# Layer two's first weights split into an attention buffer, normalised rows scaled by ScalarE and transposed two tiles later, layer one's norm weights spread by a product

## The chip, the core and the metric

The kernel runs on one core of one Trainium2 chip. TensorE (PE) multiplies matrices and transposes, VectorE (DVE), ScalarE (ACT) and GpSimd (POOL) work element by element, and SyncE (SP) issues transfers (DMA) between the chip's main memory and the core's two memories: SBUF, 128 partitions wide, and PSUM, into which PE writes. ACT can issue transfers too. Each engine runs its own list of instructions in order, and waits on semaphores for what others make. The metric is the device time of one execution in microseconds (us), as the median of several runs.

## The reference

Two equal layers work on a stream `h` of 512 tokens by 1024 columns, in float32. Each normalises its input, projects it, runs three mixers, and adds the output projection of their results to the stream.

```
def rms_norm(x, g, eps=NORM_EPS):
    xf = x.astype(jnp.float32)
    y = xf * lax.rsqrt(jnp.mean(xf * xf, axis=-1, keepdims=True) + eps)
    return (y * g.astype(jnp.float32)).astype(x.dtype)
...
    h = x
    for l in range(DEPTH):
        xn = rms_norm(h, ln_g[l])
        proj = xn @ w_in[l]
        u_a, z_a, u_b, z_b, q_lat, kv_lat, k_rope, z_c = jnp.split(proj, pts, axis=-1)
        y_a = rwkv7_mix(u_a, ...)
        y_b = rms_norm(rglru_mix(u_b, ...), lru_out_g[l])
        y_c = rms_norm(mla_mix(q_lat, kv_lat, k_rope, ...), mla_out_g[l])
        y = jnp.concatenate([y_a * jax.nn.silu(z_a), y_b * jax.nn.silu(z_b), y_c * jax.nn.silu(z_c)], axis=-1)
        h = h + y @ w_out[l]
    return rms_norm(h, final_g)
```

The change concerns `rms_norm(h, ln_g[l])` of both layers, the first columns of `xn @ w_in[l]` of layer two, and the last part of `h + y @ w_out[l]` of layer one, which overlaps them.

## The kernel before

**Precision.** Every float32 operand of a large product is split in two: a rounded high part made on ACT (`copy`, line 141) and a residue made on DVE or POOL (lines 211 and 229 for weights and activations, 306 for the normalised input). `mm3` then issues three products for each pair (lines 233, 234 and 235). A weight of 128x512 is loaded by SP into a buffer `wr` (three of them), and split by `weights` into `wH` and `wL` (four each). A `wr` is free for the next load when both parts have been made.

**Start of layer one.** The stream is cut into four tiles of 128 tokens. `LO` sets the order in which SP's first loads are written: digits are tiles of `x`, `i` the identity matrix that transposes need, `g` the norm weights `ln_g[0]`, copied to all 128 partitions (512 KB), `u`, `w`, `y` the first three weights. A scheduler sets the final order on each queue. For each tile, ACT squares two halves of 512 columns and sums them (`h_half`, line 242), ACT and DVE make 1/rms from it (`h_rstd`, lines 246, 138 and 254 to 256), DVE multiplies each half by 1/rms and by the norm weights (line 298), PE transposes it in four blocks into PSUM (line 303), ACT makes the high part `xH` (141), DVE the residue `xL` (306).

**The seam.** The last of the three output projections (`out_proj` with `final`) goes over n = 0, 1, the two halves of the 1024 columns, and in each over the four tiles. `start` loads the residual of a tile and half from main memory into `hp` (line 446, three buffers). Twelve products of four weights make the tile's result in PSUM. `finish` adds the residual (line 461, DVE), writes the sum back to main memory for the next layer's residual (464, SP), squares it (242, ACT) and multiplies it by the next norm's weights (`norm_gain`, line 286: POOL for n = 0, DVE for n = 1). After a tile's second half `norm_tile` makes 1/rms, scales both halves on DVE (line 301), and has them transposed and split as above, between the products of the tiles that are left. Layer two begins with the column groups j = 12 and j = 0, each in two halves of the tokens (`proj` with `halves`), so that the first 256-wide products need tiles 0 and 1 alone. Their four weights go through `weights` like all others.

The buffers called `am` (two of 16 KB a partition) hold the first mixer's score matrices, and later layer one's attention queries.

## Time and profile before

| | us |
|---|---|
| median of 3 runs | 857.3 (856.71 to 858.69) |
| the profiled execution | 855.86 |
| its span from the first to the last instruction | 854.0 |
| first product of layer one (PE, line 233) starts at | 15.49 |
| last-projection products stop for transposes at about | 426.3 |
| first product of layer two starts at | 434.63 |
| layer two's half-width products end at about | 449.5 |

Times in the profile are us from the span's start. A row of the timeline gives start, duration, engine, line, operation, out<-in with shapes, how many instructions were merged, and in brackets how long the engine had been idle before and what ended that. SPq is a transfer's issue on SP. `acc`, `ps` and `ck` are PSUM buffers, `c`, `g`, `sm` and `hp` SBUF buffers, `dr` main memory. The clock granted to PE was 0.984 of full on average.

### The profile page before, as it was taken

What the parts mean: (1) busy time and instruction counts of PE and PEld (TensorE: products, weight loads), DVE (VectorE), ACT (ScalarE), POOL (GpSimd) and SP (SyncE); (2) the same over time, 40 slices, a digit from 0 to 9 for tenths busy, and PEclk for the clock granted to TensorE, in tenths of its full rate; (3) what the DMA queues carried; (4) which work ended last, traced back from release to release, by engine and by line L of the source; (5) the groups of instructions that cost most, each with busy time, mean ns of one, the idle gap of its engine ahead of it and who ended that gap; (6) DMA issues with size and microseconds to landing.
All of it is one profiled execution on the core that took longest, in us unless ns stands there. A gap on an engine that the chain in (4) does not pass through costs nothing.

```text
span 854.0 us, 15206 instructions
## 1 busy us (share of the span) xinstructions
PE 796.6 (93%) x5696; PEld 621.0 (73%) x5696; DVE 571.6 (67%) x1173; ACT 506.2 (59%) x990; POOL 325.7 (38%) x299
## 2 busy tenths in 40 slices
PE   4999999999879989999989999999998799999996
PEld 4878888877559867556778788888765697675674
DVE  5678777924886496774474966695367946877736
ACT  6667885656563536574467687846575435465644
POOL 0455557513352332012344556574143523310223
PEclk9999999999999999999999999999999899999999
DMA  7222224310123365123732233332101234731354
GB/s 245 96 74 84 72 93 136 117 51 27 32 77 97 124 197 184 51 87 99 268 124 90 75 99 101 98 111 94 29 25 41 81 107 129 241 114 50 111 173 162
DMA packets 49755, 91.08 MB, mean 107 GB/s; under 512 B 5520, under 2 KB 8336, under 8 KB 49680
## 3 DMA queue, kind: packets, MB, share of 16 engines
q1 hardware_dynamic: 49104, 89.05, 32.2%
q8 instruction: 45, 0.74, 0.4%
q10 hardware_dynamic: 576, 1.05, 0.3%
q14 instruction: 30, 0.25, 0.1%
HBM read 73.30 MB, written 16.78 MB: 105 GB/s over the span
## 4 chain that ended last, share of the span: by engine, by line
PE 69%; DVE 16%; ACT 8%; issue 3%; DMA 2%; POOL 1%; SPq 1%; ACTq 0%; DVEq 0%; POOLq 0%
PE acc L233 16%; PE acc L234 16%; PE acc L235 15%; PE acc L1058 4%; PE ck L1084 3%; ACT g L138 2%; PE ps L1076 2%; PE ps L687 1%; DVE g L681 1%; PE ps L611 1%; ACT UV L141 1%; ACT L136 1%; DVE wL L229 1%; PE ps L629 1%; PE ps L786 1%
## 5 line engine op out<-in xcount | busy, mean ns | idle before, releaser
L229 POOL TENSOR_TENSOR wL<-wr,wH 128x512 fp32r<-128x512 f32 (+1 forms) x126 | 169.7, 1350 | 290.0 <-ACT wH L141 266.0
L141 ACT ACTIVATE wH<-wr 128x512 fp32r<-128x512 f32 (+1 forms) x192 | 118.8, 622 | 140.6 <-PE acc L234 74.5
L233 PE MATMUL acc<-xH,wH 128*128 128x512 f32 (+1 forms) x496 | 192.7, 390 | 0.0
L234 PE MATMUL acc<-xL,wH 128*128 128x512 f32 (+1 forms) x496 | 189.7, 383 | 0.4 <-DVE xL L306 0.2
L235 PE MATMUL acc<-xH,wL 128*128 128x512 f32 (+1 forms) x496 | 189.1, 381 | 0.0
L233 PEld LDWEIGHTS acc<-xH,wH 128*128 128x128 f32 x496 | 94.3, 191 | 18.1 <-ACT xH L141 0.7
L235 PEld LDWEIGHTS acc<-xH,wL 128*128 128x128 f32 x496 | 94.3, 190 | 17.3
L234 PEld LDWEIGHTS acc<-xL,wH 128*128 128x128 f32 x496 | 94.4, 190 | 16.9 <-DVE xL L306 0.9
L229 DVE TENSOR_TENSOR wL<-wr,wH 128x512 fp32r<-128x512 f32 (+1 forms) x66 | 49.9, 760 | 72.8 <-ACT wH L141 72.7
L233 PE MATMUL acc<-wH,c 128*128 128x512 f32 x192 | 83.0, 432 | 2.6 <-DVE hp L428 1.3
L234 PE MATMUL acc<-wL,c 128*128 128x512 f32 x192 | 77.5, 404 | 0.5 <-DVE wL L229 0.5
L235 PE MATMUL acc<-wH,c 128*128 128x512 f32 x192 | 77.1, 402 | 0.0
L141 ACT ACTIVATE UV<-ps 64x512 f32<-64x512 f32 (+4 forms) x112 | 52.4, 494 | 30.9 <-PE ps L1076 22.6
L233 PEld LDWEIGHTS acc<-wH,c 128*128 128x128 f32 x192 | 36.7, 191 | 12.8 <-ACT c L141 3.0
L141 ACT ACTIVATE c<-g 128x512 fp32r<-128x512 f32 (+1 forms) x40 | 24.9, 630 | 34.3 <-DVE g L981 22.4
L138 ACT ACTIVATE c<-acc,sm 128x128 f32<-128x128 f32 (+3 forms) x64 | 33.6, 528 | 19.1 <-DVE sm L1060 18.8
L234 PEld LDWEIGHTS acc<-wL,c 128*128 128x128 f32 x192 | 36.9, 192 | 8.6 <-issue 1.4
L1058 PE MATMUL acc<-am,am 128*128 128x128 f32 (+3 forms) x128 | 42.3, 447 | 0.8 <-ACT c L138 0.8
L235 PEld LDWEIGHTS acc<-wH,c 128*128 128x128 f32 x192 | 36.8, 192 | 8.4 <-issue 0.5
L369 POOL TENSOR_TENSOR g<-g,g 128x512 f32<-128x512 f32 x24 | 32.1, 1338 | 24.1 <-ACT g L138 24.1
L136 ACT ACT_TABLE_LOAD x31 | 39.8, 1283 | 1.3 <-PEq L1214 0.7
L138 ACT ACTIVATE g<-g 128x512 f32<-128x512 f32 (+1 forms) x58 | 36.4, 627 | 4.6 <-DVE g L705 2.6
(222 smaller groups left out, 1592.4 us busy)
## 6 DMA issues: line engine op xcount, KB each, us to landing
wr<-in_wc_dram SPq DMA_DIRECT2D x116, 256.0 KB, 2.7
wr<-in_wo_dram SPq DMA_DIRECT2D x48, 256.0 KB, 3.4
hp<-dr SPq DMA_DIRECT2D x38, 256.0 KB, 3.2
dr<-hp SPq DMA_DIRECT2D x28, 256.0 KB, 2.1
dr<-g SPq DMA_DIRECT2D x16, 256.0 KB, 2.5
g<-dr SPq DMA_DIRECT2D x16, 256.0 KB, 3.6
wr<-in_wl_dram SPq DMA_DIRECT2D x16, 208.0 KB, 2.5
dr<-c SPq DMA_DIRECT2D x12, 256.0 KB, 3.4
```

The lines of the kernel that those rows point to most:

```text
L136: chained(A.preload_act_table_set(SETS[st]))
L138: chained(A.activation(out=out, in_=in_, func=func, **kw))
L141: i = A.activation(out=out, in_=in_, func=AF.Copy, **kw)
L229: (V if wn[0] % wmod[0] == 0 or wn[0] <= 4 else G).tensor_tensor(out=L, in0=raw, in1=f(H), op=ALU.subtract)
L233: PE.matmul(o, a[0], b[0], start=start, stop=False)
L234: PE.matmul(o, a[0], b[1], start=False, stop=False)
L235: PE.matmul(o, a[1], b[0], start=False, stop=stop)
L369: G.tensor_tensor(out=z, in0=z, in1=s, op=ALU.mult)
L611: PE.matmul(os[e][:, cp, :].rearrange("p (x s) -> p x s", x=2), bk[rr, ch, :, :].rearrange("p x s -> p (x s)"), ar[rr, :, ch * 64:(ch + 1) ...
L1058: PE.matmul(o[:, 0:n], qT[:, hd, qt * 128:n], K2[:, p, e, 0:n], start=True, stop=True)
L1076: PE.transpose(o[:, (qt - kt) * 128:(qt - kt + 1) * 128], Pm[p][e, qt][:, kt * 128:(kt + 1) * 128], ident)
L1084: i = PE.matmul(ot[e * 64:(e + 1) * 64, k2 * 128:T], Vt[:, k2, 2 * p + e, :], PT[:, 2 * (k2 % 2) + e, 0:(4 - k2) * 128], start=(k2 == 0), ...
```

## The change

Four things are changed.

1. **Layer one's norm weights.** `ln_g[0]` is loaded as one row of 4 KB, issued by ACT, as is the identity matrix. Two products of a row of 128 ones (`on1`, set by POOL) with the two halves of the row spread it over 128 partitions into the two `ck` banks of PSUM, where DVE reads it in the scaling (`norm_first`). `LO` is written in another order.
2. **Layer two's first weights.** `first_weights` loads the four weights of j = 12 and j = 0 into `wr`, and splits them, high parts on ACT and residues on POOL, into one `am` buffer, before the second half of layer one's last output projection. `proj` takes them from there.
3. **Scaling.** In the seam the multiplication of a tile's two halves by 1/rms moves from DVE (`tensor_scalar`) to ACT (`copy` with a scale).
4. **Transposes.** Those of tile tt stand after the products of tile tt + 2, those of tiles 2 and 3 after all.

```diff
--- before.py
+++ after.py
@@ -61,7 +61,7 @@
     ORD1 = "M0 L0 L1 C0 M1 C1 P0 L2 O0 M2 U1 O1 C2 U2 P1 L3 M3 C3 U0 P2 O2"
     ORD2 = "G0 U3 G1 P3 G2 Z0 Z1 O3 G3 X0 f4 V0 V1 Z2 Q0 Q1 f0 V2 V3 f1 Q2 Q3 J0 f2 J1 K0 f3 W0 K1 W1 f5 W2 W3"
     ORD3 = "B0 H0 H1 A2 H2 H3 A3 H4 H5 H6 H7 B1 N0 g0 g1 t0 t6 t1 t2 t4 t5 t3 t7 T0 R0 Y0 g2 g3 T1"
-    LO = "0ig12uw3yvcm"
+    LO = "g0i1uw2y3vcm"
     Q1 = "aoooottttaaaooookvvqvkqvkqkqqqqq"
     WA, WB, WC, WD = 1000, 2, 2, 5
 
@@ -159,7 +159,8 @@
 
     vecs = P1.tile([128, DEPTH, NV], F32, name="vecs")
     cmk = g2([128, 2, 128])
-    raws, gb0 = {}, c4([128, D])
+    raws, gb0, on1 = {}, c4([128, D]), g2([1, 128])
+    G.memset(on1, 1.0)
 
     def raw_weights(j, hf):
         raws[j, hf] = tl("wr", [128, 512], F32, bufs=3)
@@ -167,10 +168,10 @@
 
 
     loads = {
-        "i": lambda: nc.sync.dma_start(out=C[:, 0:128], in_=cst[:, 0:128]),
+        "i": lambda: nc.scalar.dma_start(out=C[:, 0:128], in_=cst[:, 0:128]),
         "v": lambda: nc.sync.dma_start(out=vecs, in_=vec),
         "c": lambda: nc.sync.dma_start(out=C[:, 128:NCST], in_=cst[:, 128:NCST]),
-        "g": lambda: nc.sync.dma_start(out=gb0, in_=ln_g[0].partition_broadcast(128)),
+        "g": lambda: nc.scalar.dma_start(out=gb0[0:1, :], in_=ln_g[0].unsqueeze(0)),
         "m": lambda: nc.sync.dma_start(out=cmk, in_=cst[:, NCST + 1280:NCST + 1536].rearrange("p (a b) -> p a b", a=2)),
         "u": lambda: raw_weights(12, 0),
         "w": lambda: raw_weights(12, 1),
@@ -285,26 +286,47 @@
         hg[tt, n] = g2()
         (G, V)[n].tensor_tensor(out=hg[tt, n], in0=h[tt][:, n * 512:(n + 1) * 512], in1=xn[l][2][:, n * 512:(n + 1) * 512], op=ALU.mult)
 
-    def norm_tile(l, tt):
-
-        xH, xL, gb = xn[l]
+    def norm_first(tt):
+
+        xH, xL, gb = xn[0]
         rs = h_rstd(tt)
         c = slice(tt * 128, (tt + 1) * 128)
         for j in range(2):
             p = ps([128, 4, 128])
-            if l == 0:
-                s = slice(512 * j, 512 * j + 512)
-                src = g2()
-                V.scalar_tensor_tensor(out=src, in0=h[tt][:, s], scalar=rs, in1=gb[:, s], op0=ALU.mult, op1=ALU.mult)
-            else:
-                src = hg[tt, j]
-                V.tensor_scalar(out=src, in0=src, scalar1=rs, scalar2=None, op0=ALU.mult)
+            src = g2()
+            V.scalar_tensor_tensor(out=src, in0=h[tt][:, 512 * j:512 * j + 512], scalar=rs, in1=gb[j], op0=ALU.mult, op1=ALU.mult)
             for k in range(4):
                 PE.transpose(p[:, k, :], src[:, k * 128:(k + 1) * 128], ident)
             xh = xH[:, 4 * j:4 * j + 4, c]
             hc[tt] = copy(xh, p)
             i = V.tensor_tensor(out=xL[:, 4 * j:4 * j + 4, c], in0=p, in1=f(xh), op=ALU.subtract)
         return i
+
+    def norm_scale(tt):
+        rs = h_rstd(tt)
+        for j in range(2):
+            copy(hg[tt, j], hg[tt, j], scale=rs)
+
+    def norm_transposes(l, tt):
+        xH, xL, _ = xn[l]
+        c = slice(tt * 128, (tt + 1) * 128)
+        for j in range(2):
+            p = ps([128, 4, 128])
+            for k in range(4):
+                PE.transpose(p[:, k, :], hg[tt, j][:, k * 128:(k + 1) * 128], ident)
+            xh = xH[:, 4 * j:4 * j + 4, c]
+            copy(xh, p)
+            V.tensor_tensor(out=xL[:, 4 * j:4 * j + 4, c], in0=p, in1=f(xh), op=ALU.subtract)
+
+    wfirst = {}
+
+    def first_weights(l):
+        W = tl("am", [128, 4, 2, 512], F32R, bufs=2)
+        for i, (j, hf) in enumerate(((12, 0), (12, 1), (0, 0), (0, 1))):
+            raw = tl("wr", [128, 512], F32, bufs=3)
+            nc.sync.dma_start(out=raw, in_=wc[l, j, :, 4 * hf:4 * hf + 4, :].rearrange("p k c -> p (k c)"))
+            split(raw, W[:, i, 0, :], W[:, i, 1, :], G)
+            wfirst[l, j, hf] = W[:, i, 0, :], W[:, i, 1, :]
 
     ov = out.rearrange("(n p) d -> p n d", p=128)
 
@@ -332,7 +354,8 @@
 
             if halves:
                 o = acc()
-                W = [weights(wc[l, j, :, 4 * hf:4 * hf + 4, :].rearrange("p k c -> p (k c)"), raw=raws.pop((j, hf), None)) for hf in range(2)]
+                W = [wfirst.pop((l, j, hf), None) or weights(wc[l, j, :, 4 * hf:4 * hf + 4, :].rearrange("p k c -> p (k c)"), raw=raws.pop((j, hf), None))
+                     for hf in range(2)]
                 for th in range(2):
                     t = slice(th * 256, (th + 1) * 256)
                     for k in range(8):
@@ -467,15 +490,22 @@
                         h_half(tt, n)
                         norm_gain(l + 1, tt, n)
                         if n == 1:
-                            norm_tile(l + 1, tt) if l + 1 < depth else final_tile(tt)
+                            norm_scale(tt) if l + 1 < depth else final_tile(tt)
 
                 if final and n == 1:
                     W = [weights(wo[l, m, n, :, k, :]) for k in range(4)]
+                    if l + 1 < depth:
+                        first_weights(l + 1)
                     for tt in range(4):
                         start(tt)
                         for k in range(4):
                             mm(tt, k, W[k])
                         finish(tt)
+                        if tt >= 2 and l + 1 < depth:
+                            norm_transposes(l + 1, tt - 2)
+                    if l + 1 < depth:
+                        for tt in (2, 3):
+                            norm_transposes(l + 1, tt)
                 else:
                     for tt in range(4):
                         start(tt)
@@ -1116,11 +1146,15 @@
 
         out_proj(2, [ysplit(y) for y in yc], lambda: mix_rstd(token_sums(stc), rsqrt_ln), True)
 
-    norm_start(0, gb0)
+
+    go = [ck(), ck()]
+    for n in range(2):
+        PE.matmul(go[n], on1, gb0[0:1, n * 512:(n + 1) * 512], start=True, stop=True)
+    norm_start(0, go)
     for tt in range(4):
         for n in range(2):
             h_half(tt, n)
-        last_v = norm_tile(0, tt)
+        last_v = norm_first(tt)
         behind += [hc[tt]] * BN[tt]
         if tt == 3:
             with tc.issue_after(getattr(last_v, "ins", last_v)):
```

**Place one: the start, SP's queue.** Here `c4` are the tiles of x, `wr` weights, `C` the identity. Before:

```order
L158 DMA c4_3_71<-in_x_dram 128x512 x2
L170 DMA C_67<-in_cst_dram 128x128
L173 DMA c4_2_70<-in_ln_g_dram 128x1024
L158 DMA c4_4_76<-in_x_dram 128x512 x2
L158 DMA c4_5_79<-in_x_dram 128x512 x2
L166 DMA wr_6_82<-in_wc_dram 128x512
```

With the change:

```order
L167 DMA wr_6_81<-in_wc_dram 128x512
L158 DMA c4_4_74<-in_x_dram 128x512 x2
L158 DMA c4_5_78<-in_x_dram 128x512 x2
L167 DMA wr_7_83<-in_wc_dram 128x512
L158 DMA c4_8_85<-in_x_dram 128x512 x2
```

The identity and the norm weights have left the queue, and the scheduler has put the first weight ahead of tile 0.

**Place two: entry of the seam, ACT and SP.** From the split of the out-projection's third weight of the second half (`wr_890` before, `wr_891` now) on. L242 and L243 are squares of the first half's tiles, `wr_893` and `wr_894` the fourth weight, `am` layer two's weights. ACT before:

```order
L141 ACTIVATE wH_891_4387<-wr_890_4385 128x512
L242 ACTIVATE g2_867_4342,sm_866_4341<-c4_864_4337 128x512
L242 ACTIVATE g2_872_4351,sm_871_4350<-c4_869_4346 128x512
L141 ACTIVATE wH_894_4393<-wr_893_4391 128x512
L242 ACTIVATE g2_877_4360,sm_876_4359<-c4_874_4355 128x512
L242 ACTIVATE g2_882_4369,sm_881_4368<-c4_879_4364 128x512
```

ACT with the change:

```order
L141 ACTIVATE wH_892_4391<-wr_891_4389 128x512
L141 ACTIVATE am_897_4401<-wr_898_4402 128x512
L243 ACTIVATE g2_868_4346,sm_867_4345<-c4_865_4341 128x512
L243 ACTIVATE g2_873_4355,sm_872_4354<-c4_870_4350 128x512
L243 ACTIVATE g2_878_4364,sm_877_4363<-c4_875_4359 128x512
L141 ACTIVATE wH_895_4397<-wr_894_4395 128x512
L141 ACTIVATE am_897_4401<-wr_899_4406 128x512
L243 ACTIVATE g2_883_4373,sm_882_4372<-c4_880_4368 128x512
L141 ACTIVATE am_897_4401<-wr_900_4410 128x512
L141 ACTIVATE am_897_4401<-wr_901_4414 128x512
L243 ACTIVATE g2_905_4436,sm_867_4345<-c4_865_4341 128x512
```

SP's queue in the same place, where `hp` are residual loads and `dr` the sums written back. `hp_847` and `hp_848` are the first half's tile 3, `hp_896` and `hp_902` the second half's tile 0. Before:

```order
L221 DMA wr_942_4597<-in_wc_dram 128x512
L221 DMA wr_945_4603<-in_wc_dram 128x512
L446 DMA hp_847_4249<-dr_781_4000 128x512
L464 DMA dr_865_4339<-c4_864_4337 128x512
L464 DMA dr_870_4348<-c4_869_4346 128x512
L464 DMA dr_875_4357<-c4_874_4355 128x512
L446 DMA hp_896_4397<-dr_810_4104 128x512
L464 DMA dr_880_4366<-c4_879_4364 128x512
L446 DMA hp_906_4444<-dr_821_4159 128x512
```

With the change:

```order
L327 DMA wr_898_4402<-in_wc_dram 128x512
L327 DMA wr_899_4406<-in_wc_dram 128x512
L469 DMA hp_848_4253<-dr_782_4004 128x512
L487 DMA dr_866_4343<-c4_865_4341 128x512
L487 DMA dr_871_4352<-c4_870_4350 128x512
L487 DMA dr_876_4361<-c4_875_4359 128x512
L327 DMA wr_900_4410<-in_wc_dram 128x512
L487 DMA dr_881_4370<-c4_880_4368 128x512
L327 DMA wr_901_4414<-in_wc_dram 128x512
L469 DMA hp_902_4418<-dr_811_4108 128x512
L469 DMA hp_910_4451<-dr_822_4163 128x512
L469 DMA hp_918_4484<-dr_829_4199 128x512
```

On ACT a split of layer two's first weight has come between two splits of the out-projection and ahead of three squares, and three more before the second half's squares. On SP two more weight loads and the write of the first half's tile 3 stand ahead of the second half's first residual load. POOL makes the four new residues between its four multiplications of `norm_gain`, and DVE's residue of the fourth weight stands, as before, ahead of the first half's tile 3.

**Place three: the seam's second half, ACT.** L138 with `sm` are the steps of 1/rms, `ps` transposed blocks. Before, from the square of tile 1's second half to the first xH of tile 1:

```order
L242 ACTIVATE g2_909_4462,sm_871_4350<-c4_869_4346 128x512
L138 ACTIVATE sm_912_4468<-sm_911_4466 128x1
L138 ACTIVATE sm_912_4468<-sm_912_4468 128x1
L141 ACTIVATE wH_943_4599<-wr_942_4597 128x512
L242 ACTIVATE g2_919_4509,sm_876_4359<-c4_874_4355 128x512
L141 ACTIVATE wH_946_4605<-wr_945_4603 128x512
L141 ACTIVATE xH_839_4238<-ps_904_4428 128x4x128
L141 ACTIVATE xH_839_4238<-ps_905_4436 128x4x128
L138 ACTIVATE sm_922_4515<-sm_921_4513 128x1
L141 ACTIVATE wH_956_4675<-wr_955_4673 128x512
L138 ACTIVATE sm_922_4515<-sm_922_4515 128x1
L141 ACTIVATE xH_839_4238<-ps_914_4475 128x4x128
```

With the change, from the square of tile 0's second half to the first xH of tile 0:

```order
L243 ACTIVATE g2_905_4436,sm_867_4345<-c4_865_4341 128x512
L243 ACTIVATE g2_913_4469,sm_872_4354<-c4_870_4350 128x512
L138 ACTIVATE sm_908_4442<-sm_907_4440 128x1
L141 ACTIVATE wH_959_4738<-wr_958_4736 128x512
L138 ACTIVATE sm_908_4442<-sm_908_4442 128x1
L141 ACTIVATE wH_962_4756<-wr_961_4754 128x512
L243 ACTIVATE g2_921_4502,sm_877_4363<-c4_875_4359 128x512
L138 ACTIVATE sm_916_4475<-sm_915_4473 128x1
L141 ACTIVATE g2_869_4348<-g2_869_4348,sm_908_4442 128x512
L141 ACTIVATE g2_906_4438<-g2_906_4438,sm_908_4442 128x512
L138 ACTIVATE sm_916_4475<-sm_916_4475 128x1
L141 ACTIVATE xH_840_4242<-ps_926_4517 128x4x128
```

Behind this, ahead of tile 1's first xH, now stand the square of tile 3, tile 0's second xH, one weight split, four scalings of tiles 1 and 2, and three small steps. Squares and splits of later tiles have come ahead of the scaling of earlier ones. On PE all 48 products of the second half now stand in one run, ahead of the first transposes.

## The prediction

> **What bounds the kernel now.** I read the page first: one core, TensorE (PE) busy 93% of the span, and on the chain that ended last for 69%.
>
> ```profile
> span 854.0 us, 15206 instructions
> PE 796.6 (93%) x5696; PEld 621.0 (73%) x5696; DVE 571.6 (67%) x1173; ACT 506.2 (59%) x990; POOL 325.7 (38%) x299
> PE 69%; DVE 16%; ACT 8%; issue 3%; DMA 2%; POOL 1%; SPq 1%; ACTq 0%; DVEq 0%; POOLq 0%
> ```
>
> So the change can pay only where PE stands still, or cost only where it makes PE stand still. It touches two such places. PE's groups of instructions from 398 to 452 us, the seam between the layers (after the second bar the idle us before them and who ended it), and from PE's list of waits from 0 to 30 us the start (total us, times, longest):
>
> ```profile
> L303 PE MATMUL ps<-C,g 128*128 128x128 f32 x32 | 5.1, 295 | 4.6 <-DVE xL L306 2.5 <-DVE g L301 1.6 <-DVE sm L254 0.5
> L234 PE MATMUL acc<-wL,c 128*128 128x512 f32 x39 | 15.4, 396 | 0.5 <-DVE wL L229 0.5
> PE ps L303 <- DVE g L298: 11.9, 3, 8.9
> ```
>
> The seam costs PE 4.6 + 0.5 = 5.1 us of waiting, the start 8.9 us before its first instruction.
>
> **The start.** The timeline of the first 16 us, and the window from 8 to 12 us, whose last number is the GB/s that the DMA engines moved:
>
> ```profile
> 0.74 0.86 SPq L158 DMA_DIRECT2D c<-in_x_dram  x2
> 3.87 0.63 ACT L242 ACTIVATE g<-c 128x512 f32<-128x512 f32 x1 [1.86 <-DMA c<-in_x_dram]
> 6.32 0.16 DVE L256 SCALAR_TENSOR_TENSOR sm<-sm,sm 128x1 f32<-128x1 f32 x1
> 8.09 1.42 DVE L298 SCALAR_TENSOR_TENSOR g<-c,sm,c 128x512 f32<-128x512 f32 x2 [1.61 <-DMA c<-in_ln_g_dram]
> 12.82 1.41 DVE L298 SCALAR_TENSOR_TENSOR g<-c,sm,c 128x512 f32<-128x512 f32 x2
> 15.49 0.58 PE L233 MATMUL acc<-xH,wH 128*128 128x256 f32 x1
> 8.00:12.00 4.00, 1.97 (x8) 1.57 (x8) 2.86 (x7) 3.31 (x9) 0.00 (x0) 1.00 1.06 403
> ```
>
> Tile 0's 1/rms is there at 6.48, but its scaling waits until 8.09 for the 512 KB copy of the norm's weights. From there to the first product at 15.49 (7.40 us) every link is an instruction order: tile 1's scaling at 12.82 stands on DVE behind tile 0's residues and a weight's.
>
> Now the copy is one 4 KB row on ScalarE's queue, spread by two PE products, so that wait goes. But SyncE's first load is now a 256 KB weight, ahead of x. One load more costs 0.43 us to issue (0.86 for two) and, at 403 GB/s, 0.65 us to move; I take 0.8. So 1/rms comes at 7.3, and the scaling starts there: **-0.8 us**, with the 7.40 us behind it unchanged. The ends: 0, if x loses 1.6 (both loads of a pair late) or the row lands late, and -1.6, the whole wait, since x cannot come sooner than now. The two products and their landing I cost at nothing: the cover is the stretch to 7.3; a row issued by 1.2 that lands like x (3.1 after issue: 0.74 to 3.87) leaves 3.0 us for two products (nearest kind below, 0.6 us each, double when the clock is slow).
>
> ```profile
> L1058 PE MATMUL acc<-am,am 128*128 128x512 f32 x32 | 15.8, 605 | 0.0
> ```
>
>  Reading the weights from PSUM instead of SBUF costs 0.04 us an instruction (L461 0.75, L298 0.71), within the ends. Ident on the other queue hides too: nothing needs it before the scaled rows.
>
> **The seam, entry.** The timeline of before:
>
> ```profile
> 414.03 3.08 SPq L221 DMA_DIRECT2D wr<-in_wc_dram  x2
> 414.75 0.63 ACT L141 ACTIVATE wH<-wr 128x512 fp32r<-128x512 f32 x1 [1.37 <-DMA wr<-in_wo_dram]
> 415.37 0.63 ACT L242 ACTIVATE g<-c 128x512 f32<-128x512 f32 x1
> 416.03 0.64 ACT L242 ACTIVATE g<-c 128x512 f32<-128x512 f32 x1
> 416.66 0.62 ACT L141 ACTIVATE wH<-wr 128x512 fp32r<-128x512 f32 x1
> 417.31 1.25 DVE L229 TENSOR_TENSOR wL<-wr,wH 128x512 fp32r<-128x512 f32 x1 [0.66 <-ACT wH L141]
> 418.95 0.40 PE L235 MATMUL acc<-wH,c 128*128 128x512 f32 x1
> 419.18 0.40 PE L233 MATMUL acc<-wH,c 128*128 128x512 f32 x1
> 419.13 0.94 SPq L446 DMA_DIRECT2D hp<-dr  x1
> 420.86 0.75 DVE L461 SCALAR_TENSOR_TENSOR c<-acc,sm,hp 128x512 f32<-128x512 f32 x1 [2.30 <-DMA hp<-dr]
> 423.42 0.75 DVE L461 SCALAR_TENSOR_TENSOR c<-acc,sm,hp 128x512 f32<-128x512 f32 x1 [1.81 <-DMA hp<-dr]
> ```
>
> The DMA list, asked at 414.0 (layer two's first weight), 419.1 and 421.9 (residual loads), gives the time from issue to landing at the end:
>
> ```profile
> wr<-in_wc_dram SPq DMA_DIRECT2D x1, 256.0 KB, 3.2
> hp<-dr SPq DMA_DIRECT2D x1, 256.0 KB, 4.2
> hp<-dr SPq DMA_DIRECT2D x1, 256.0 KB, 3.0
> ```
>
> Before, the weight of 414.03 waits for its split until the out-projection's second half is under way. Now that split stands on ScalarE right behind the one of 414.75, ahead of three squares and of the split of the last out-projection weight. It lands at 417.2, so ScalarE waits from 415.4, and the last split starts at 417.25 + 0.63 + 3 x 0.65 = 419.8 instead of 416.66: +3.1. Its residue on DVE, which took 1.25 there, ends at 421.65 instead of 418.56. PE, which waits 0.5 there now, stands some 2.6 us and then 0.5; that alone is free, because the 35 products left end at 421.65 + 35 x 0.23 (the starts of 418.95 and 419.18) = 429.7, before anything after them is ready. What pays is the queue behind it: DVE's fourth first-half result (420.86) stands behind that residue: 421.65 to 422.4. SyncE writes it out, and only behind that write and another weight load come the second half's residual loads: the first at about 423.25, not 419.13. With 3.2 us (between 3.0 and 4.2) it lands at 426.45, so the result of 423.42 comes at 426.45: **+3.05**.
>
> **The seam, second half.** Before, from there to layer two's first product:
>
> ```profile
> 425.21 0.44 ACT L138 ACTIVATE sm<-sm 128x1 f32<-128x1 f32 x2 [0.23 <-DVE sm L246]
> 427.49 0.87 DVE L301 TENSOR_SCALAR g<-g,sm 128x512 f32<-128x512 f32 x2
> 427.91 3.37 POOL L229 TENSOR_TENSOR wL<-wr,wH 128x512 fp32r<-128x512 f32 x2
> 428.28 1.27 DVE L254 TENSOR_TENSOR sm<-sm 128x1 f32<-128x1 f32 x1
> 428.87 1.06 ACT L141 ACTIVATE xH<-ps 128x512 fp32r<-128x512 f32 x2
> 434.63 0.78 PE L233 MATMUL acc<-xH,wH 128*128 128x256 f32 x2
> 841.38 0.72 ACT L141 ACTIVATE g<-g,sm 128x512 f32<-128x512 f32 x1 [0.68 <-DVE sm L256]
> 434.63:449.50 14.87, 14.86 (x115) 14.61 (x114) 8.08 (x20) 9.43 (x18) 5.23 (x6) 0.91 0.36 111
> ```
>
> 423.42 to 434.63 is 11.2 us, most of it DVE. Now the eight scalings leave DVE (0.44 each at 427.49) for ScalarE (0.72 each, the row of the final norm at 841.38), and ScalarE's own queue sets the pace. From the first square (427.2) to tile 1's first xH it holds 4 squares at 0.65, 3 weight splits and 2 xH at about 0.55 (two xH in 1.06), 6 scalings at 0.65 when they follow each other, 7 small ones at 0.22: 10.8 us, so 438.0. It must also wait: 0.5 for PE's first transposes, and for DVE's small steps, which stand up to 1.27 us beside a busy POOL (428.28 beside 427.91); I take 0.7. xH from 439.2, the first product at 439.8: **+5.2** for the whole seam. The ends: +2.5 (residual load at 2.6 us, no waits, 0.5 per instruction) and +6.5 (4.2 us, two stalls, PSUM buffers late). From there 14.87 us of products as now; four transposes now wait for buffers, within the ends.
>
> The page GPSIMD Engine Reference of the Trainium skill (Specifications) has POOL share SBUF interfaces with DVE "in a 2-port perf mode or with two SBUF inputs". Were DVE's scalings alone in contention with POOL, the stalls would leave with them and the sum would be 0.7 lower, 861.0. By the page the small steps contend through their own two inputs, and the trace agrees: L254, with two inputs and 128x1, is the row that stood 1.27 us. I keep the 0.7.
>
> **The sum.** Later products stand in nearly the same order and the weights stay ahead: 0, within 0.7 either way. -0.8 + 5.2 = +4.4 on the profiled execution, 855.86 us (854.0 of span and 1.9 around it): 860.3. The median of the runs, 857.3, stands 1.4 above that execution: **861.7**.
>
> **Rivals.**
> *It does what its parts promise* (faster). The weights are split before they are needed, the out-projection runs unbroken, and all of the seam's 5.1 us and the 0.8 go: 851.4. For it: PE's longest waits there are the chain the change relieves. It decides if layer two's first weight lands before ScalarE reaches it, at 415.4; against it: issued at 414.03, landing 3.2 later, and nothing ahead of it in the queue is moved.
> *The late entry is won back on DVE* (same). Without scalings (8 x 0.44 = 3.5) and stalls (1.27) the second half could shorten by 4.8, so 5.2 - 4.8 - 0.8 = -0.4: 856.9. It needs ScalarE not to be the longer queue; the count of 10.8 us against 11.2 now speaks against it.
> *PE goes slow in the gap* (slower still). After its 2.46 us wait PE ran slowly for a while, as these rows show: starts 0.22 apart, while the whole stretch's 115 instructions in 14.87 us mean 0.13.
>
> ```profile
> 432.74 0.66 PE L303 MATMUL ps<-C,g 128*128 128x128 f32 x4 [2.46 <-DVE xL L306]
> 435.51 0.42 PE L235 MATMUL acc<-xH,wL 128*128 128x256 f32 x1
> 435.73 0.41 PE L233 MATMUL acc<-xH,wH 128*128 128x256 f32 x1
> ```
>
> If the new 2.6 us wait at 417.7 did that to the out-projection and it stayed slow to its end, 35 products at 0.39 (0.23 x 0.22 / 0.13) would end at 435.3, 2.4 after the transposes are wanted (432.9, at the end of tile 0's scaling by the count above): 864.1. TensorE: Matmul & The Clock Gate of the Trainium skill (Part 1) asks for an idle window of about 3.4 us before the clock halves; by that this wait is too short, and the gap of 430 to 439 costs one slow stretch as now.
>
> **How the numbers follow.** My case 0.70 (859.0 to 863.8), won back on DVE 0.13, faster 0.08, slow clock 0.09. A measurement of this kernel tells about 0.2%, 1.7 us, from no change: slower 0.79, same 0.13, faster 0.08. The range 857.0 to 864.5 leaves out the faster case, about half of the second and part of the last.
>
> **What would show it.** Right: ScalarE idle some 1.9 us before the first am copy, for a weight DMA; PE waiting about 3 us for wH and wL of the last out-projection weight; the second half's first residual load issued at 423; layer two's first product about 13 us after the result it feeds. Scaling of tile 0 at the start near 7.3, with no wait for the norm weights. Wrong: no ScalarE wait at the first am copy, or the first product of layer two less than 22 us after the load of 414.03 (20.6 before, 25.8 by my sum) would contradict the seam; an x load that lands like before would make the start worth 1.6.

## The result, and the profile after

The changed kernel is slower: 870.5 us median (868.75 to 871.4) against 857.6 (856.71 to 858.69) of the kernel before, a ratio of 1.0147 with a 95% interval of 1.0126 to 1.0169. Times 858 us, the ratio gives +12.6 us (the medians lie 12.9 apart), where +4.4 was forecast. The direction was right, the forecast size a third of the true one. The page of the changed kernel, beside that of before: a span of 869.6 us instead of 854.0, and TensorE busy for 11 us longer although it has only four instructions more.

```profile
span 869.6 us, 15214 instructions
PE 807.7 (93%) x5700; PEld 627.2 (72%) x5700; DVE 571.3 (66%) x1164; ACT 510.4 (59%) x998; POOL 324.9 (37%) x301
PE 69%; DVE 16%; ACT 8%; issue 3%; DMA 2%; POOL 1%; SPq 0%; ACTq 0%; DVEq 0%; POOLq 0%
```

More busy time for the same work means a slower clock: the mean granted clock is 0.973 of full, 0.984 before. Where the 15.6 us of span come from is read by the same events in both traces:

| event | before | after | gained since the row above |
|---|---|---|---|
| SyncE's load of layer two's norm weights (L152) | 404.93 | 406.48 | +1.55 |
| first 512-wide product of layer two (half-width products done) | 449.44 | 460.23 | +9.24 |
| first write of a bonus term of layer two (`dr<-g`, L598, L628 after) | 498.39 | 512.51 | +3.33 |
| the next such write | 507.17 | 521.96 | +0.67 |
| end of the span | 854.0 | 869.6 | +0.8 |

**The seam.** The timeline of the changed kernel, to be laid beside the rows of before (take 1.55 off for what was late already):

```profile
419.29 0.63 ACT L141 ACTIVATE am<-wr 128x512 fp32r<-128x512 f32 x1 [1.94 <-DMA wr<-in_wc_dram]
421.67 0.61 ACT L141 ACTIVATE wH<-wr 128x512 fp32r<-128x512 f32 x1
422.33 0.89 PE L234 MATMUL acc<-wH,c 128*128 128x512 f32 x2 [1.85 <-ACT wH L141]
422.97 0.74 DVE L484 SCALAR_TENSOR_TENSOR c<-acc,sm,hp 128x512 f32<-128x512 f32 x1
424.10 0.42 SPq L327 DMA_DIRECT2D wr<-in_wc_dram  x1
424.58 1.40 SPq L469 DMA_DIRECT2D hp<-dr  x3
429.90 1.41 DVE L484 SCALAR_TENSOR_TENSOR c<-acc,sm,hp 128x512 f32<-128x512 f32 x2 [6.20 <-DMA hp<-dr]
433.16 0.94 DVE L255 TENSOR_TENSOR sm<-sm 128x1 f32<-128x1 f32 x1
434.13 1.26 DVE L256 SCALAR_TENSOR_TENSOR sm<-sm,sm 128x1 f32<-128x1 f32 x1
436.16 1.33 ACT L141 ACTIVATE g<-g,sm 128x512 f32<-128x512 f32 x2 [1.75 <-DVE sm L257]
436.93 1.97 PE L316 MATMUL ps<-C,g 128*128 128x128 f32 x8 [3.83 <-ACT g L141]
441.14 1.97 PE L316 MATMUL ps<-C,g 128*128 128x128 f32 x8 [2.24 <-ACT g L141]
444.15 0.80 PE L234 MATMUL acc<-xH,am 128*128 128x256 f32 x2 [1.04 <-ACT xH L141]
```

The DMA list, asked at 424.9 to 425.2, has the time from issue to landing of the second and third residual load at its end:

```profile
hp<-dr SPq DMA_DIRECT2D x2, 256.0 KB, 5.4
```

In the trace of before one residual load, issued right behind two weight loads, took even longer. The rows of SyncE's queue, and that of the DMA list, asked at 403.9 to 404.3:

```profile
403.01 0.88 SPq L221 DMA_DIRECT2D wr<-in_wo_dram  x2
403.98 0.38 SPq L446 DMA_DIRECT2D hp<-dr  x1
```

```profile
hp<-dr SPq DMA_DIRECT2D x1, 256.0 KB, 6.0
```

The reader sees the forecast chain link by link: ScalarE waits 1.94 us for the first early weight, the last output weight is split late, VectorE's fourth first-half result comes at 422.97, and SyncE issues the residual loads only behind that result's write and a fourth weight load. Two links are longer than forecast. The residual lands 5.3 us after its issue (424.58 to 429.90), not 3.2. And TensorE runs at half its clock. The windows of the changed kernel show that (us of the window, its length, then busy time of PE, PEld, DVE, ACT, POOL, then the granted clock, the share of the DMA engines and GB/s):

```profile
419.34:422.76 3.42, 1.57 (x7) 0.96 (x7) 0.45 (x1) 3.42 (x9) 3.39 (x4) 1.00 0.79 254
433.00:436.41 3.41, 0.10 (x1) 0.00 (x0) 3.41 (x7) 1.45 (x5) 2.38 (x4) 1.00 0.82 259
436.41:439.82 3.41, 1.97 (x8) 1.57 (x8) 1.65 (x6) 2.91 (x9) 0.10 (x1) 0.50 0.92 276
439.82:443.24 3.42, 1.97 (x8) 1.57 (x8) 2.27 (x7) 2.93 (x7) 1.27 (x1) 0.50 0.31 101
443.24:446.65 3.41, 2.50 (x11) 2.28 (x12) 2.49 (x5) 3.07 (x8) 1.38 (x2) 0.50 0.16 55
446.65:450.06 3.41, 3.41 (x18) 3.41 (x18) 2.07 (x3) 2.01 (x4) 1.12 (x1) 0.50 0.02 5
450.06:453.47 3.41, 3.41 (x31) 3.41 (x30) 2.12 (x4) 2.80 (x4) 0.00 (x0) 1.00 0.00 0
444.15:460.23 16.08, 16.08 (x113) 15.85 (x113) 9.00 (x13) 9.56 (x16) 2.60 (x3) 0.82 0.06 17
```

These windows are not chosen freely. All changes of the clock in a trace lie on one grid of 3.41 us, and a window with less than some 1.4 us of TensorE's recorded work is followed by a slow one, one with 1.4 to 1.6 mostly (counts in the last section). Before, one slow window stood in the seam (433.9 to 437.3); now four stand there in a row, and the half-width products take 16.08 us instead of 14.87 (row of before in the prediction).

**Behind the seam.** The third row of the table, +3.3 us, lies 30 to 50 us behind the edit. VectorE's and TensorE's rows of before, and of the changed kernel:

```profile
477.38 0.74 DVE L499 SCALAR_TENSOR_TENSOR g<-acc,omu,hp 128x512 f32<-128x512 f32 x1
478.05 1.12 DVE L593 SCALAR_TENSOR_TENSOR g<-g,vecs,g 128x512 f32<-128x512 f32 x1
479.98 0.49 PE L525 MATMUL ps<-c,bones 128*128 128x512 f32 x1 [0.54 <-ACT c L141]
```

```profile
488.64 1.58 DVE L623 SCALAR_TENSOR_TENSOR g<-g,vecs,g 128x512 f32<-128x512 f32 x1
490.14 0.74 DVE L529 SCALAR_TENSOR_TENSOR g<-acc,omu,hp 128x512 f32<-128x512 f32 x1
492.73 0.49 PE L555 MATMUL ps<-c,bones 128*128 128x512 f32 x1 [2.48 <-ACT c L141]
```

The two instructions of VectorE have changed places (L593 is L623 after, L499 is L529). No line of the diff touches them; the scheduler put them so. The blend of a column group (L529) now stands behind a bonus product that is wanted later, ScalarE's square of it comes late, and TensorE waits 2.48 us for the head sums instead of 0.54. Behind that wait stands another slow window.

### The profile page after: what moved, and what is told of

It is laid out like the page before. It is cut to its first block, busy times and chain, and to the rows that moved or that the text cites. A ratio compares the mean times of both kernels' runs of the same rounds, so it can differ in the third digit from the quotient of the medians.

```text
span 869.6 us, 15214 instructions
## 1 busy us (share of the span) xinstructions
PE 807.7 (93%) x5700; PEld 627.2 (72%) x5700; DVE 571.3 (66%) x1164; ACT 510.4 (59%) x998; POOL 324.9 (37%) x301
## 4 chain that ended last, share of the span: by engine, by line
PE 69%; DVE 16%; ACT 8%; issue 3%; DMA 2%; POOL 1%; SPq 0%; ACTq 0%; DVEq 0%; POOLq 0%
PE acc L234 16%; PE acc L235 15%; PE acc L236 15%; PE acc L1088 4%; PE ck L1114 3%; ACT g L138 3%; PE ps L1106 2%; PE ps L717 2%; PE ps L641 1%; ACT UV L141 1%; DVE g L711 1%; DVE c L212 1%; PE ps L659 1%; PE ps L816 1%; ACT wH L141 1%
## 5 line engine op out<-in xcount | busy, mean ns | idle before, releaser
L230 POOL TENSOR_TENSOR wL<-wr,wH 128x512 fp32r<-128x512 f32 (+1 forms) x123 | 165.0, 1344 | 305.8 <-ACT wH L141 289.4
L141 ACT ACTIVATE wH<-wr 128x512 fp32r<-128x512 f32 (+1 forms) x188 | 116.1, 621 | 141.9 <-PE acc L235 74.2
L234 PE MATMUL acc<-xH,wH 128*128 128x512 f32 (+1 forms) x464 | 184.1, 397 | 0.0
L235 PE MATMUL acc<-xL,wH 128*128 128x512 f32 (+1 forms) x464 | 181.1, 390 | 0.4 <-DVE xL L302 0.2
L236 PE MATMUL acc<-xH,wL 128*128 128x512 f32 (+1 forms) x464 | 180.2, 389 | 0.0
L234 PEld LDWEIGHTS acc<-xH,wH 128*128 128x128 f32 x464 | 88.4, 191 | 18.1 <-ACT xH L141 0.5
L235 PEld LDWEIGHTS acc<-xL,wH 128*128 128x128 f32 x464 | 88.8, 191 | 16.9 <-DVE xL L302 0.9
L236 PEld LDWEIGHTS acc<-xH,wL 128*128 128x128 f32 x464 | 88.5, 191 | 17.1
L138 ACT ACTIVATE c<-acc,sm 128x128 f32<-128x128 f32 (+3 forms) x64 | 33.6, 527 | 18.8 <-DVE sm L1090 18.7
L138 ACT ACTIVATE g<-g 128x512 f32<-128x512 f32 (+1 forms) x58 | 36.4, 627 | 4.7 <-DVE g L735 2.6
```

Source lines behind the costliest of these rows:

```text
L138: chained(A.activation(out=out, in_=in_, func=func, **kw))
L141: i = A.activation(out=out, in_=in_, func=AF.Copy, **kw)
L230: (V if wn[0] % wmod[0] == 0 or wn[0] <= 4 else G).tensor_tensor(out=L, in0=raw, in1=f(H), op=ALU.subtract)
L234: PE.matmul(o, a[0], b[0], start=start, stop=False)
L235: PE.matmul(o, a[0], b[1], start=False, stop=False)
L236: PE.matmul(o, a[1], b[0], start=False, stop=stop)
```

## Experiments

Each difference below is the ratio to the kernel before on the same chip, less one, times 858 us, with its 95% interval. The profile gives for some of them how long after the load of layer two's norm weights (first row of the table above) four events come:

| kernel | time, us against before | tile 0's second result | first half-width product | first 512-wide product | first bonus write |
|---|---|---|---|---|---|
| before | 0 | 18.49 | 29.70 | 44.51 | 93.46 |
| changed | +12.6 (10.8 to 14.5) | 23.42 | 37.67 | 53.75 | 106.03 |
| e1_start | -0.9 (-2.1 to +0.2) | 18.27 | 29.34 | 44.56 | 93.54 |
| e2_weights | +12.0 (10.0 to 14.2) | 22.92 | 37.12 | 52.54 | 104.79 |
| e3_scale | +3.6 (2.2 to 5.0) | 18.39 | 28.81 | 46.83 | 95.14 |
| e4_late | +1.6 (0.5 to 2.7) | 17.93 | 30.54 | 46.16 | 94.46 |
| i1_no_weights | +5.1 (3.4 to 6.8) | 18.46 | 28.36 | 48.67 | 97.64 |
| f1_residual | +5.3 (3.5 to 7.1) | 19.15 | 30.41 | 45.61 | 100.15 |
| f2_order | +11.0 (8.9 to 13.0) | 22.96 | 37.20 | 53.34 | 103.58 |
| f3_warm | +11.2 (8.8 to 13.6) | 21.98 | 35.36 | 49.26 | 104.83 |
| f4_swap | +5.8 (3.8 to 7.9) | 19.29 | 30.60 | 45.38 | 100.16 |
| h2_swap_fill | +1.3 (-0.1 to 2.7) | 18.91 | 30.20 | 44.86 | 94.29 |
| g1_both | +3.7 (2.3 to 5.0) | 18.69 | 29.40 | 44.61 | 97.25 |
| h3_both_fill | +3.8 (2.4 to 5.2) | 18.46 | 29.63 | 44.84 | 96.71 |

### One part of the change at a time

**The start alone (e1_start).** Its diff is the start's part of the change:

```diff
-    LO = "0ig12uw3yvcm"
+    LO = "g0i1uw2y3vcm"
...
-        "g": lambda: nc.sync.dma_start(out=gb0, in_=ln_g[0].partition_broadcast(128)),
+        "g": lambda: nc.scalar.dma_start(out=gb0[0:1, :], in_=ln_g[0].unsqueeze(0)),
...
+        PE.matmul(go[n], on1, gb0[0:1, n * 512:(n + 1) * 512], start=True, stop=True)
```

> The kernel before with the start alone changed (norm row on ScalarE's queue, spread by two products, first loads in the new order); seam as before. The forecast's theory: -0.8 us. What the trace of the changed kernel shows if its start is the rule: +1.0 us, all of it from the clock, which rose at 19.9 instead of 17.4. Rival, that the instant at which the clock rises falls anywhere within some 3.4 us from execution to execution: the scaling is 0.3 to 0.4 us earlier as in the changed kernel, the median moves by -0.4 with an error of about 1, and this profile shows another instant.

Measured: -0.9 (-2.1 to +0.2). That the start would lose time is refuted, and -0.8 and 0 stay possible. In its trace the scaling of tile 0 starts at 8.18, in the changed kernel's at 7.75, in that of before at 8.09: the wait for the norm weights is gone, but x lands later, by about as much in this trace and by most of it in the changed kernel's. The first 512-wide product of layer one shows how far executions of one start lie apart. These rows are of the kernel before, and of f4_swap, which has the same start:

```profile
31.32 0.40 PE L233 MATMUL acc<-xH,wH 128*128 128x512 f32 x1
```

```profile
33.65 0.40 PE L233 MATMUL acc<-xH,wH 128*128 128x512 f32 x1
```

They are 2.3 us apart with nothing changed. Two things make that up. The copy of the norm weights landed later in f4_swap, so that tile 0's scaling starts at 9.22 instead of 8.09 and the first product at 16.61 instead of 15.49. And TensorE came to its full clock later: the window from 17.43 to 20.85 holds 32 products before and 16 in f4_swap. The load of the first table's first row comes at 404.6 to 408.0 in the nine traces with the start of before, so nothing can be read from its +1.55 about the change.

**The early weights alone (e2_weights).**

```diff
+                    if l + 1 < depth:
+                        first_weights(l + 1)
                     for tt in range(4):
                         start(tt)
```

> The kernel before with layer two's first four weights split into the am buffer ahead of the last half projection, and nothing else: scalings on VectorE, transposes in place. Theory A, that the late entry carries the loss: at least +5 us, ScalarE waiting some 3 us for weights at the first am copies, the first residual load of the second half some 4 us late. Rival B, that the second half's queue on ScalarE carries it: +1 to +3 us, since the short second half on VectorE stays as it was.

Measured: +12.0, as much as all four parts together, with scalings on VectorE and transposes in place as before. Its rows are the changed kernel's over again:

```profile
425.14 1.40 SPq L457 DMA_DIRECT2D hp<-dr  x3
430.41 0.75 DVE L472 SCALAR_TENSOR_TENSOR c<-acc,sm,hp 128x512 f32<-128x512 f32 x1 [6.14 <-DMA hp<-dr]
```

The residual of tile 0 lands 5.3 us after its issue, tile 0's second result is 4.4 us late, the first half-width product 7.4. Theory A holds and rival B is out, though A's marks were only near: ScalarE waits 1.5 us for the first early weight, not 3, and the first residual load is issued 3.4 us late against the load of the norm weights, not 4.

**The scalings alone (e3_scale), the late transposes alone (e4_late).**

```diff
-                V.tensor_scalar(out=src, in0=src, scalar1=rs, scalar2=None, op0=ALU.mult)
+                copy(src, src, scale=rs)
```

> The kernel before with the seam's eight scalings on ScalarE instead of VectorE, and nothing else. Theory A: within 1 us of the kernel before. Rival B: +3 us or more, the first product of layer two later than 11.2 us after the result of tile 0's second half.

```diff
-                            norm_tile(l + 1, tt) if l + 1 < depth else final_tile(tt)
+                            norm_scale(tt) if l + 1 < depth else final_tile(tt)
...
+                        if tt >= 2 and l + 1 < depth:
+                            norm_transposes(l + 1, tt - 2)
```

> The kernel before with the seam's transposes two tiles later, and nothing else (scalings on VectorE). Theory A: within 1 us of the kernel before, since the transposes' results are wanted only by layer two. Rival B: +2 us or more, by the buffers that four tiles' transposes wait for and by a longer stand of TensorE with a slow clock behind it. The part's promise: the out-projection runs to its end without a stop and the seam is 1 to 2 us shorter.

Measured: +3.6 and +1.6. Both theories had part of it wrong. With scalings on ScalarE the first product comes 10.4 us after the result (28.81 - 18.39), not later than the 11.2 of before; what is lost comes behind it, where the half-width products take 18.0 us (46.83 - 28.81) instead of 14.8. With the late transposes the first product is 0.8 us late, and 0.8 more goes in the products. Neither brings what its part promises.

**The changed kernel without the early weights (i1_no_weights).**

```diff
-                    if l + 1 < depth:
-                        first_weights(l + 1)
```

> The changed kernel without the early split of layer two's first weights: they go through the common buffers as before; start, scalings on ScalarE and late transposes as changed. If the parts add up (start -0.9, scalings +3.6, transposes +1.6 by the kernels with one part each): +4.3 us over the kernel before. Theory, that the early split alone makes the loss, and that ScalarE's scalings and late transposes, which cost by themselves, fit together: 0 to +2 us.

Measured: +5.1. The three other parts add up (their sum was +4.3); that they fit together is refuted. Its half-width products take 20.3 us (48.67 - 28.36), those of f1_residual below, which has the early weights and the same other parts, 15.2. So beside these three parts the early weights help the products of the seam by some 5 us, once the residuals are not late. The gain does not show in the time (f1_residual, which has the swapped pair behind its seam, stands at +5.3), and the kernel before, without early weights, needs only 14.8. Nor do the costs add up: +12.0 for the early weights alone and +5.1 for the other three would make 17, not 12.6.

### Why the early weights cost so much

**Residual loads ahead of them (f1_residual).** In the changed kernel:

```diff
+                        for tt in range(3):
+                            residual(tt)
                         first_weights(l + 1)
```

> The changed kernel with the residual loads of the second half's first three tiles written ahead of layer two's first weights: on SyncE's queue the third and fourth of these weights then stand behind them. Nothing else is moved. Theory A1, that the residual loads' late issue sets the end of the seam: tile 0's second result 3 to 4 us earlier against the loads of the seam's start, and the kernel at +8 to +10 us over the kernel before instead of +12 to +13. Rival A2, that ScalarE's queue, where the four splits stand, holds the chain whatever the residuals do: the result comes earlier, the first product of layer two does not, and the time stays at +12 to +13.

Measured: +5.3, so 7 us of the loss are gone. The rows of SyncE, VectorE and TensorE:

```profile
419.85 0.91 SPq L470 DMA_DIRECT2D hp<-dr  x1
424.11 0.75 DVE L488 SCALAR_TENSOR_TENSOR c<-acc,sm,hp 128x512 f32<-128x512 f32 x1 [1.67 <-DMA hp<-dr]
435.37 0.50 PE L234 MATMUL acc<-xH,am 128*128 128x256 f32 x2
```

The last output weight is split as late as in the changed kernel (419.95, where before had 416.66), but the residual load is issued at 419.85, before the third and fourth weight, and from result to first product it takes 11.26 us, as before (11.2). The seam ends 1.1 us later than before instead of 9.2. Theory A1 holds and went further than it said: writing the residual loads first takes away 8.1 of the 9.2 us at the seam. Tile 0's second result itself comes 4.3 us earlier. Another 3.0 go between it and the first product, but the forecast's count of ScalarE's queue there (13.35 us) is not tested by this, because the scheduler made another list for ScalarE: four scalings and two weight splits stand between the square of tile 0 and tile 1's first xH, six and three in the changed kernel.

The rest of the loss lies behind the seam, where the first bonus write is 6.7 us late (100.15 against 93.46). The pair on VectorE is swapped here too, with the same wait, and three slow windows follow from 485.4 to 495.6:

```profile
482.98 0.51 PE L561 MATMUL ps<-c,bones 128*128 128x512 f32 x1 [2.46 <-ACT c L141]
```

By their traces the pair is swapped in e2_weights as well, and in none of e1_start, e3_scale, e4_late and i1_no_weights. The seam of i1_no_weights is 4.2 us late, that of f1_residual 1.1. So the swap comes with the early weights, and not with a late seam.

**Residuals early in the kernel before (g2_early, h1_early_behind), and in the changed one (g4_early_all).** If late residuals cost, early ones might gain. They were loaded into a free `am` buffer:

```diff
+                        R = tl("am", [128, 4, 512], F32, bufs=2)
+                        for tt in range(4):
+                            hps[tt] = R[:, tt, :]
+                            nc.sync.dma_start(out=hps[tt], in_=hsrc[tt, n])
                     W = [weights(wo[l, m, n, :, k, :]) for k in range(4)]
```

(In h1_early_behind the new lines stand behind the last one.)

> The kernel before with the four residuals of the second half loaded into an am buffer as soon as the first half's projections have written them, instead of through the three hp buffers; nothing else. Theory, that the residual loads carry the seam in the kernel before too (results of 420.86 and 423.42 wait 2.3 and 1.8 us for them): tile 0's second result 2 to 3.5 us earlier, TensorE's 4.6 us of waiting at the transposes shorter by half or more, 2 to 5 us faster than the kernel before. Rival: the norms on VectorE and ScalarE set the pace, and the time moves by less than 1 us.

> The kernel before with the second half's four residuals in an am buffer, as in the kernel with early residuals, but written behind the four loads of its output weights, so that these are not late. Theory, that the earlier try lost only what SyncE's queue took from the weights: faster than the kernel before by 1 to 4 us. Rival, that early results of the second half run into the norms of the first half on VectorE and ScalarE: within 1 us, or slower.

> The changed kernel with all its parts, the residuals loaded early into the other am buffer, and the pair on VectorE in the old order. If the late residuals alone stood between the weights' early split and its promise, this is the fastest of all: 3 to 6 us faster than the kernel before. Rival, that the four splits in ScalarE's queue and the scalings there cost by themselves: 0 to +4 us.

Measured: +3.2 (2.0 to 4.4), +4.6 (2.6 to 6.6) and +6.5 (5.4 to 7.6): all slower than before, and the theories are out. Of the rivals only that of h1_early_behind allowed for it; the other two lost more than theirs said. In the first the four loads stood ahead of three output weights on SyncE, and ScalarE waited 5.16 us for the first of these. In the second they did not, tile 0's second result came 1.2 us earlier, and it gained nothing. In its trace tile 1's norm falls beside POOL's three weight residues, as VectorE's row and POOL's row of h1_early_behind show; that this is the reason was not tried by itself.

```profile
433.36 2.92 DVE L301 TENSOR_SCALAR g<-g,sm 128x512 f32<-128x512 f32 x2
```

```profile
433.07 4.33 POOL L229 TENSOR_TENSOR wL<-wr,wH 128x512 fp32r<-128x512 f32 x3 [8.56 <-ACT wH L141]
```

Two scalings that took 0.87 us in the kernel before took 2.92. GPSIMD Engine Reference of the Trainium skill (Specifications) names contention with VectorE instructions in a 2-port mode or with two SBUF inputs; the scaling has one large input, and whether it runs in that mode no run here shows.

### The pair on VectorE, and the clock

**The pair put back (f2_order), and swapped in the kernel before (f4_swap).**

```diff
-            V.scalar_tensor_tensor(out=bo, in0=r, scalar=vc("r_k", p), in1=k, op0=ALU.mult, op1=ALU.mult)
+            i = V.scalar_tensor_tensor(out=bo, in0=r, scalar=vc("r_k", p), in1=k, op0=ALU.mult, op1=ALU.mult)
+            if l == 1 and p == 0:
+                tc.add_manual_dep(getattr(i, "ins", i), getattr(blend[5], "ins", blend[5]).name, NOSYNC, reason="issue order")
```

(f4_swap has the two instructions of the last line the other way round, in the kernel before.)

> The changed kernel with one pair on VectorE in layer two put back in the order that it has in the kernel before (the blend of the sixth column group ahead of the bonus product of the first head pair), some 35 us behind the seam. Theory: the wait of 2.5 us before the head sums falls to about 0.5, the slow clock behind it goes, and the kernel stands at +9 to +10 us over the kernel before instead of +12 to +13. Rival: the wait is carried by what stands ahead of both on VectorE (stalls beside GpSimd), and the time moves by less than 1 us.

> The kernel before with that one pair on VectorE in layer two put in the changed kernel's order, and nothing else. Theory: TensorE waits 2.5 us instead of 0.5 before the head sums, runs a window at the slow clock behind it, and the kernel is 2 to 4 us slower than the kernel before. Rival: less than 1 us, the order follows the lateness and does not make it.

Measured: +11.0 and +5.8. Put back in the changed kernel, the stretch from the first 512-wide product to the bonus write shrinks from 52.3 to 50.2 us in the trace (48.95 before), and the wait falls from 2.48 to 0.80, but the time moves by less than its error. Swapped in the kernel before, the pair costs 5.8 (3.8 to 7.9), at or above the top of the 2 to 4 expected. The two waits there are 1.2 us longer together (1.87 and 0.48 instead of 0.54 and 0.60); the windows of f4_swap show that the clock goes slow behind them:

```profile
482.12:485.53 3.41, 1.54 (x7) 0.87 (x5) 1.96 (x3) 1.72 (x3) 3.41 (x5) 1.00 0.24 77
485.53:488.95 3.42, 2.94 (x19) 2.27 (x19) 2.01 (x3) 3.03 (x7) 2.93 (x5) 0.50 0.36 119
488.95:492.36 3.41, 3.41 (x17) 2.85 (x16) 2.58 (x4) 3.33 (x5) 0.00 (x0) 0.50 0.12 42
492.36:495.77 3.41, 3.41 (x14) 2.99 (x14) 1.94 (x4) 1.20 (x2) 0.00 (x0) 0.50 0.00 0
495.77:499.18 3.41, 3.41 (x9) 2.63 (x9) 2.00 (x3) 0.13 (x1) 0.00 (x0) 0.50 0.00 0
499.18:502.60 3.42, 3.42 (x16) 2.81 (x16) 2.40 (x4) 1.77 (x4) 1.03 (x2) 1.00 0.21 57
```

Behind the wait of 1.87 us TensorE ran at half its clock for 13.6 us, through three windows in which its record shows it busy throughout. Why it came back so late no run shows: in the changed kernel one slow window follows the same place.

**The same swap with the wait filled (h2_swap_fill).** Eight products that nobody reads, ahead of the head sums:

```diff
+            for _ in range(fill):
+                i = PE.matmul(o, bones, xH[:, 0, :], start=True, stop=True)
             i = PE.matmul(o, bones, H, start=True, stop=False)
```

> The kernel before with the one pair on VectorE swapped, and 8 products that nobody reads in the wait of 1.9 us that this makes ahead of the head sums. Theory, that the swap's 5 to 7 us are mostly the slow clock that the wait sets off (four windows of 3.4 us in its profile): +1 to +3 us over the kernel before, no slow stretch at 485. Rival, that the order itself delays the work behind it: +5 us or more with or without a slow clock.

Measured: +1.3, not told apart from nothing. The windows of h2_swap_fill at that place:

```profile
482.05:485.46 3.41, 2.84 (x25) 1.94 (x24) 2.83 (x4) 3.22 (x8) 3.32 (x4) 1.00 0.26 79
485.46:488.88 3.42, 3.26 (x22) 2.48 (x22) 3.01 (x6) 3.35 (x5) 0.22 (x2) 1.00 0.28 81
```

The order on VectorE is still the bad one, and 4.5 of its 5.8 us are gone with the slow clock. (The products also moved a few later instructions of VectorE.) So, as far as this run shows, most of what the swap costs is the slow clock.

**The seam's gaps filled in the changed kernel (f3_warm).** The edit also writes all transposes behind the last product, fixes their order, and adds three products behind tile 1's:

```diff
+            for tt, d in enumerate((13, 8, 0, 0)):
+                if d:
+                    lastpe[0] = fill_gap(d, lastpe[0], y[0][:, 0, 0:128], W[0][0])
                 norm_transposes(l + 1, tt)
```

> The changed kernel with 24 products whose result nobody reads in TensorE's gaps of the seam (13 before the transposes of tile 0, 8 before those of tile 1, 3 behind them). Theory C, that TensorE's slow clock from 436 to 450 is part of the loss: the transposes of a tile take 1.2 us instead of 2.0, the first half-width products start at the fast pace, and the kernel stands at +9 to +10.5 us over the kernel before. Rival: the chain over ScalarE sets the pace of the half-width products, and the time moves by less than 1 us.

Measured: +11.2, inconclusive by the time alone. In the trace theory C holds at its place: no slow window in the seam, and it is 4.5 us shorter (first 512-wide product at 49.26 instead of 53.75). Of these, 1.4 stand already at tile 0's second result, ahead of the fill, so some 3 us go with the slow clock. The gain is given back behind it: four slow windows follow the wait at the head sums instead of one, and the bonus write stands at 104.83.

**Both repairs (g1_both), and with a fill at the head sums (h3_both_fill).** The edits of f1_residual and f2_order together, then with four such products as in h2_swap_fill.

> The changed kernel with both repairs: the residual loads of three tiles ahead of the first weights, and the one pair on VectorE in the old order. Theory, that these two and the slow clock behind them are nearly all of the loss: 0 to +2.5 us over the kernel before. Rival, that the loss is given back elsewhere as soon as one cause goes: +4 us or more.

> The changed kernel with both repairs (residual loads ahead, the pair in the old order) and 4 products that nobody reads ahead of the same head sums. Theory, that what is left of the loss after both repairs (+3.7 us) is the slow clock from 484 to 494: within 1.5 us of the kernel before. Rival: it stays at +3 us or more.

Measured: +3.7 and +3.8. The seam of both is that of before (44.61 and 44.84 against 44.51), so the residual loads account for the seam's loss. Against f1_residual the pair's old order brings the first bonus write 2.9 us earlier in the trace, while the time (+3.7 against +5.3) moves by less than its error. What remains stands behind the seam again: slow windows from 484.4 to 494.5 after waits of only 0.8 and 0.6 us in g1_both, from 486.6 to 493.4 in h3_both_fill, where a new wait of 1.5 us for VectorE came up. The theory of h3_both_fill failed as tried; that remainder is open.

### Looking for a version that beats both

**Early residuals with the new start (g3_early_start); the gap of the seam filled in the kernel before (i2_seam_fill), and with the new start (i3_start_fill).**

```diff
+                        for _ in range(9):
+                            i = PE.matmul(o, y[0][:, 0, 0:128], W[0][0], start=True, stop=True)
```

> The same with the changed kernel's start. If the start is worth 0 to 0.4 us, as the kernel with the start alone showed, this stands within 1 us of the kernel with early residuals alone; the forecast's theory has it 0.8 us faster.

> The kernel before with 9 products that nobody reads in TensorE's wait of 2.46 us in the seam, ahead of the transposes of tile 1. Theory, that this wait sets off the slow clock which its profile shows from 433.9 to 437.3: no slow stretch there, first half-width products at the fast pace, 1 to 2 us faster than the kernel before. Rival, that what follows there waits for the norms anyway: within 0.7 us.

> The same with the changed kernel's start, the one part that did not cost anything by itself: the candidate to beat both kernels. By the sum of the two, 1.5 to 3 us faster than the kernel before; by the rival, within 1 us of it.

Measured: +2.2 (1.3 to 3.3), +3.2 (2.0 to 4.3) and +2.2 (1.2 to 3.3). Both kernels with the start stand 1.0 us under their twins without it, which fits e1_start. The fill lost: the scheduler ordered ScalarE's seam anew around it, and a wait that before did not have came up in i2_seam_fill (total us, times, longest):

```profile
PE acc L233 <- ACT xH L141: 2.8, 1, 2.8
```

None beats the kernel before by more than the error; the new start alone, at 0.9989 (0.9975 to 1.0002), is the nearest.

## Why the prediction came out as it did

- **The start, -0.8.** Within the interval of the start alone (-2.1 to +0.2), and the two pairs of twins, 1.0 us apart, point the same way. The forecast scaling at 7.3 was 7.75 in the changed kernel, so the step "x loses 0.8" was too small there: x lost 1.15 (its first square at 5.02 instead of 3.87).
- **The seam's entry, +3.05.** The mechanism was right link by link, and these marks came: ScalarE's wait 1.94 (1.9 forecast), the last split at 420.1 on the clock of before (419.8), the residue's end at 421.5 (421.65), the first residual load at 423.0 (423.25). ScalarE's wait came out so near partly by luck: the load of layer two's first weight was issued 1.1 us late against before (416.71, less 1.55, instead of 414.03) and landed in 2.6 us, not 3.2, while the prediction had nothing ahead of it moved. The step "with 3.2 us (between 3.0 and 4.2) it lands at 426.45" failed: 5.3 us, with two of the new weight loads and a write under way when it was issued. The trace of before held a nearer row, the load of 403.98 shown above, with 6.0. The result was 4.9 us late, not 3.05. TensorE's own wait (1.85 for wH and none for wL, about 3 forecast) was free, as claimed: the out-projection ended at 433.1, and the transposes were wanted at 436.9.
- **The seam's second half, +2.15.** It was +3.05 (14.25 us from result to first product, against 13.35 forecast and 11.2 before), and layer two's first product came 27.4 us after its first weight's load (416.71), where the sum had 25.8. The stated cause, that ScalarE's own queue sets the pace, held in part. From its first square to tile 1's first xH (430.75 to 443.52, 12.8 us) it worked 9.8 and waited 2.9, where the sum had 10.8 and 1.2. The mis-sized term is the waiting: 1.75 of it ended with VectorE's small steps, two of which stood 0.94 and 1.26 where 0.7 was put in, and TensorE's transposes ran at half clock (1.97 for eight, 1.10 before).
- **"14.87 us of products as now".** 16.08, by the four slow windows. The first premise, that the change can cost only where it makes TensorE stand still, left out what its clock does afterwards. The rival that TensorE goes slow in the gap had named the mechanism, but weighed it for the out-projection alone, where the slow window (422.8 to 426.1) indeed cost nothing. By TensorE: Matmul & The Clock Gate of the Trainium skill (Part 1), which asks for about 3.4 us of idling, the forecast wait of 2.6 us was called too short. The trace disagrees: the wait was 1.85 us, and the window of 419.34 with 1.57 us of work in 3.42 was followed by a slow one. That the page calls its window free-running agrees with the grid.
- **"Later products stand in nearly the same order: 0, within 0.7 either way."** This is the step that failed most: 4.0 us between the first 512-wide product and the second bonus write, 0.8 later. The order that changed was VectorE's. Alone, in the kernel before, the swapped pair costs 5.8 us, mostly by the clock; inside the changed kernel putting it back moved the time by 1.6, less than its error, so its share of the 4.8 stays open, as does what is left of the loss in g1_both (+3.7).
- **The rival that was put as faster** needed the weights to land before ScalarE reached them. They did not, but f1_residual shows that it was not the point: with the last output weight split as late, the seam was nearly as short as before once the residual loads no longer stood behind the third and fourth weight.

Together: 9.2 instead of 5.2 at the seam and 4.8 instead of 0 behind it, on a start that measurement cannot tell from the one forecast.

## What to carry to other kernels

When loads are written earlier, read the issuing queue for what now stands behind them and is wanted sooner; here four early weights alone cost 12 us, as much as the whole change, and 7 of the change's 12.6 came back when the residual loads were written ahead of them. Compare the order on every engine for 50 us behind an edit, not only on the one that bounds the kernel, since a scheduler may swap a pair that the diff never names. And price a wait of TensorE by what the clock does after it: in f4_swap 1.2 us more of waiting cost 5.8, of which 4.5 went when the wait was filled.
